# Second feed-forward net of a two-layer encoder: one more pair of blocks in seven-product form, and the down projection of eight inner blocks as seven products over both halves of the sequence

## The chip, the cores and the metric

The kernel runs on one core of one Trainium2 chip. Its time is the device time of one execution in microseconds. The core has a matrix engine (TensorE, PE in the profile), a vector engine (DVE), a scalar engine (ACT), GpSimd (POOL) and SyncE (SP), which here only issues transfers (DMAs). Each engine works through its own list of instructions in order.

## The reference

A sequence of 1024 rows of width 1024 passes through two layers and a final norm:

```
for layer in range(2):
    h = h + mixer(rms_norm(h, mix_norm[layer]))       # layer 0: gated mixing and pooling; layer 1: RWKV-7
    h = h + swiglu(rms_norm(h, ffn_norm[layer]), w_gate[layer], w_up[layer], w_down[layer])
return rms_norm(h, final_norm)

swiglu(x) = (silu(x @ w_gate) * (x @ w_up)) @ w_down      # 1024 -> 2816 -> 1024
```

The RWKV-7 mixer carries a state along the sequence, chunk by chunk; it is called the recurrence here. Everything is float32.

## The kernel before

**Tiles.** Activations lie transposed: 128 features by 512 positions is a tile, so the sequence has two halves (h = 0 and 1), the width has 8 tiles (m) and the inner width of 2816 has 22 blocks (f), or 11 pairs of blocks (i = 0 to 10). Every float32 operand is split in two parts, hi and lo, and a product of 128 x 128 by 128 x 512 is three matmuls (hi·hi, lo·hi, hi·lo): lines 441 to 443 (`mm3`) and 777 to 779 (`quarter`, four such products). A split costs one copy on ACT (`whi`, L161) and one subtraction on DVE (`wlo`, L162).

**Weights** are fetched in a fixed list (`plan`, filled by `push`, emptied by `take`), 512 KB at a time on ACT's queue, and split ahead of use. `dests` names where the split parts go; `whl` is the ordinary pair of buffers.

**Seven-product form.** Gate and up projections of most pairs are computed as a 2 x 2 block product with seven products in place of eight: the 2 x 2 is two halves of the inputs' features and two halves of the sequence (columns), and the weights' four quarters (a11 to a22) are combined on DVE (`weights` in `full_steps`: s1 to s4), as are the inputs (t1 to t4). Combining the inputs is done once for all pairs: in `combine1`, four steps, each of four loads of stored normed rows (`rl`, L2262), four subtractions (`rt`, L2267) and four splits into the tiles of `x["t1"]` to `x["t4"]`, beside the plain products of `plain_b`. A product that needs the first half alone (`first1`) is made early, beside the recurrence, and its result kept in `p1_d`.

**The second net, in order of time.** (1) The recurrence of the second half of the sequence, 1562 to 1760 us: its small matmuls wait for each other through DVE and ACT, and `drive` interleaves dense work between them: gate and up of the last of the first half's blocks, their downs, and the first products (`first1`) of four units (`AHEAD_IN`; a unit is the gate or the up of a pair). At its end the recurrence normalises (`ysb`, with a reciprocal root on POOL, `var` L446) and turns its outputs (`sm<-ident,ysb`). (2) Two more units of `first1`, the mixer's output projection, the other units. (3) `plain_b`, 1845 to 1957: gate and up of the second half for blocks 0 to 9 (pairs 0 to 4), beside `combine1`. (4) `full_steps(UNITS, ...)`, 1957 to 2124: pairs 5 to 10 in seven-product form for both halves. The hidden blocks go out to `hid1_d`. (5) `last_downs`, 2124.5 to 2317: the down projection by pairs of blocks, both halves for pairs 5 to 10, the second half alone for pairs 0 to 4 (the first half's were done beside the recurrence). Each tile of outputs is one PSUM bank, filled by 6 matmuls and added to the resident h by DVE (`residual`, L540: `h<-h,mm` for the second half, `ahi<-ahi,mm` for the first, which lies in an old tile of that name). Five PSUM banks rotate. The second half's h is brought back from `hs_d` at the stage's start (`reload`, L1960). (6) The last pair is done by `final_down` with outputs by rows, then the final norm.

A scheduler sets each engine's list of instructions at build time, so the order on DVE and SP beside PE's is fixed. All engine lists are the same as before up to a point in the recurrence of the second half at about 1690 us; everything moved lies behind that.

## Time and profile before

| | us |
|---|---|
| median of 3 runs | 2331.52 (2330.39 to 2339.88) |
| profiled execution, its own time | 2329.14 |
| its span in the profile | 2327.4 |
| PE busy | 2270.2 (98%) |
| DVE busy | 1547.3 (66%) |
| ACT busy | 957.1 (41%) |
| last stage (5), 2124.5 to 2317 | 192.5 |
| end of the last matmul stage to end of span | 10.4 |

The profile counts an engine as busy while an instruction of it runs; matmuls overlap each other, so the duration of one (389 ns in the table of lines) is longer than the distance between two starts. Idle time of PE is followed by an arrow and the engine and tile that ended it.

### The profile page before, as it was taken

How to read it: one execution, taken by the hardware profiler on the slowest of the kernel's cores; microseconds unless marked ns; L12 is line 12 of the kernel's file. 1: busy time of each engine (PE TensorE's matmuls, PEld its weight loads, DVE VectorE, ACT ScalarE, POOL GpSimd, SP SyncE). 2: the span in 40 equal slices, each digit the busy share in tenths (PEclk: the TensorE clock that was granted, in tenths of full speed). 3: DMA queues.
4: the chain of work that ended last, by engine and by line, in shares of the span. 5: the costliest groups of instructions: out<-in, count | busy, mean ns of one | idle time of the engine just before them, and what ended most of it. 6: DMA issues, size and time to landing. Idle time of an engine off the chain costs nothing.

```text
span 2327.4 us, 37995 instructions
## 1 busy us (share of the span) xinstructions
PE 2270.2 (98%) x15171; PEld 1855.4 (80%) x15171; DVE 1547.3 (66%) x2500; ACT 957.1 (41%) x1527; POOL 181.7 (8%) x207
## 2 busy tenths in 40 slices
PE   8999999999999999999998999998999999999998
PEld 6888888888888788787786788786778888888886
DVE  6435775656567976875778957775766665776565
ACT  6233444434223665533345765532333442332024
POOL 0200000000000012110110011200100000000002
PEclk9999999999999999999998999999999999999999
DMA  5114473332676466786545376775557674546342
GB/s 180 53 46 145 136 204 118 99 127 95 252 250 223 143 198 156 190 242 172 173 136 157 117 217 158 196 240 157 165 154 231 224 235 133 177 156 255 127 164 98
DMA packets 427393, 389.70 MB, mean 167 GB/s; under 512 B 99280, under 2 KB 358480, under 8 KB 424272
## 3 DMA queue, kind: packets, MB, share of 16 engines
q1 hardware_dynamic: 183120, 206.09, 27.7%
q10 hardware_dynamic: 241664, 173.30, 25.1%
q0 software_dynamic: 2432, 7.88, 1.3%
q8 instruction: 119, 1.95, 0.3%
q14 instruction: 58, 0.48, 0.1%
HBM read 281.15 MB, written 106.04 MB: 166 GB/s over the span
## 4 chain that ended last, share of the span: by engine, by line
PE 80%; DVE 11%; DMA 5%; issue 2%; ACT 1%; POOL 1%; SPq 0%; ACTq 0%; POOLq 0%; DVEq 0%
PE mm L441 14%; PE mm L442 14%; PE mm L443 14%; PE mm L777 9%; PE mm L779 9%; PE mm L778 9%; PE sm L1573 4%; DVE wlo L162 2%; DVE it L1513 1%; DVE xi L1518 1%; PE yp L1573 1%; DMA raw<-in_ffn_w_gate_dram 1%; PE mm L627 1%; PE mm L628 1%; PE mm L629 1%
## 5 line engine op out<-in xcount | busy, mean ns | idle before, releaser
L161 ACT ACTIVATE whi<-raw 128x1024 fp32r<-128x1024 f32 (+2 forms) x274 | 265.0, 975 | 401.5 <-PE mm L442 201.5
L162 DVE TENSOR_TENSOR wlo<-raw,whi 128x1024 fp32r<-128x1024 f32 (+2 forms) x274 | 307.8, 1128 | 154.3 <-ACT whi L161 119.9
L442 PE MATMUL mm<-alo,whi 128*128 128x512 f32 x864 | 341.4, 395 | 1.6 <-DVE alo L162 0.8
L441 PE MATMUL mm<-ahi,whi 128*128 128x512 f32 x832 | 331.0, 399 | 0.5 <-ACT whi L161 0.5
L443 PE MATMUL mm<-ahi,wlo 128*128 128x512 f32 x832 | 327.6, 394 | 0.5 <-DVE wlo L162 0.5
L540 DVE TENSOR_TENSOR h<-h,mm 128x512 f32<-128x512 f32 x268 | 180.2, 684 | 130.8 <-PE mm L443 127.7
L777 PE MATMUL mm<-ahi,whi 128*128 128x512 f32 x536 | 210.5, 393 | 2.3 <-DVE t L905 1.4
L778 PE MATMUL mm<-alo,whi 128*128 128x512 f32 x536 | 208.7, 389 | 0.0
L779 PE MATMUL mm<-ahi,wlo 128*128 128x512 f32 x536 | 205.3, 390 | 0.0
L442 PEld LDWEIGHTS mm<-alo,whi 128*128 128x128 f32 x864 | 162.9, 189 | 37.8 <-issue 2.6
L443 PEld LDWEIGHTS mm<-ahi,wlo 128*128 128x128 f32 x832 | 156.8, 189 | 36.0 <-issue 2.5
L441 PEld LDWEIGHTS mm<-ahi,whi 128*128 128x128 f32 x832 | 157.0, 189 | 35.5 <-issue 1.9
L441 PE MATMUL mm<-hd,dhi 128*128 128x512 f32 x368 | 144.3, 392 | 1.0 <-DVE h L540 1.0
L443 PE MATMUL mm<-hd,dlo 128*128 128x512 f32 x368 | 143.4, 390 | 0.0
L442 PE MATMUL mm<-hd,dhi 128*128 128x512 f32 x368 | 143.2, 389 | 0.0
L777 PEld LDWEIGHTS mm<-ahi,whi 128*128 128x128 f32 x536 | 100.6, 188 | 25.6 <-issue 3.2
L779 PEld LDWEIGHTS mm<-ahi,wlo 128*128 128x128 f32 x536 | 100.6, 188 | 21.1
L778 PEld LDWEIGHTS mm<-alo,whi 128*128 128x128 f32 x536 | 100.6, 188 | 21.0 <-issue 0.5
L161 ACT ACTIVATE dhi<-raw 128x1024 fp32r<-128x1024 f32 x40 | 40.6, 1053 | 170.8 <-PE mm L442 131.3
L161 ACT ACTIVATE hid<-t 128x512 fp32r<-128x512 f32 x58 | 36.5, 629 | 115.0 <-DVE t L875 113.3
L441 PEld LDWEIGHTS mm<-hd,dhi 128*128 128x128 f32 x368 | 69.1, 188 | 16.1 <-DVE h L540 1.6
L443 PEld LDWEIGHTS mm<-hd,dlo 128*128 128x128 f32 x368 | 69.1, 188 | 14.4
(446 smaller groups left out, 4706.2 us busy)
## 6 DMA issues: line engine op xcount, KB each, us to landing
raw<-in_ffn_w_down_dram ACTq DMA_DIRECT2D x76, 512.0 KB
raw<-in_ffn_w_gate_dram ACTq DMA_DIRECT2D x68, 512.0 KB
raw<-in_ffn_w_up_dram ACTq DMA_DIRECT2D x68, 512.0 KB
hid_d<-hid SPq DMA_DIRECT2D x68, 512.0 KB
hd<-hid_d SPq DMA_DIRECT2D x56, 512.0 KB
ar<-ab_d SPq DMA_DIRECT2D x16, 1024.0 KB
raw<-in_ab_w_in_dram ACTq DMA_DIRECT2D x16, 512.0 KB
raw<-in_ab_w_out_dram ACTq DMA_DIRECT2D x16, 512.0 KB
```

The source lines that it names most:

```text
L161: act.activation(hi, src, AF.Copy)
L162: (eng or dve).tensor_tensor(out=lo, in0=src, in1=hi.bitcast(F32), op=ALU.subtract)
L441: pe.matmul(o, whi, xhi, start=first, stop=False)
L442: pe.matmul(o, whi, xlo, start=False, stop=False)
L443: newest[0] = pe.matmul(o, wlo, xhi, start=False, stop=last).ins
L540: dve.tensor_tensor(out=H[h][:, m, :], in0=H[h][:, m, :], in1=o, op=ALU.add)
L627: pe.matmul(ops[j], xhi[:, k, sl], whi[:, kk], start=(k == 0), stop=False)
L628: pe.matmul(ops[j], xhi[:, k, sl], wlo[:, kk], start=False, stop=False)
L777: pe.matmul(o, wh[:, k, :], x[0][:, k, :], start=st, stop=False, skip_group_check=True)
L778: pe.matmul(o, wh[:, k, :], x[1][:, k, :], start=False, stop=False, skip_group_check=True)
L779: pe.matmul(o, wl[:, k, :], x[0][:, k, :], start=False, stop=k == 3, skip_group_check=True)
L1573: i = f(*args, **kw)
```

## The change

Pair 4 (blocks 8 and 9) joins the seven-product pairs (`LATER`), so `plain_b` covers blocks 0 to 7 only, `full_steps` takes 14 units and not 12, the first half's blocks 8 and 9 leave the dense work beside the recurrence, and two units of `first1` are made there in addition (`AHEAD_IN` 6). The down projection of the last stage is rearranged: first pair 8 (`EARLY_D`) in the old form for both halves, then blocks 0 to 7 for the second half by columns of the weights (`four_downs`: one PSUM bank takes four blocks, 12 matmuls), then blocks 8 to 15 for both halves as seven products (`eight_downs`), then pair 9 and, as before, the last pair in `final_down`. The seven-product part needs combinations of the hidden blocks 8 to 15: `keep_hidden` writes these blocks unsplit to `hf_d`, and `combine2` loads them, four at a time, into the old tiles chi and clo, subtracts and splits; `drive` interleaves it with the early downs. Hidden blocks are loaded four at a time (`load_four`).

```diff
-LATER = (5, 6, 7, 8, 9, 10)
-AHEAD_IN = 4
+LATER = (4, 5, 6, 7, 8, 9, 10)
+AHEAD_IN = 6
...
+    def keep_hidden(h, f, s, to):
+        if to is hid1_d and F4 <= f < F4 + 8:
+            sp.dma_start(hf_d[h][:, f - F4], s)
...
-        for fd in range(2 * LATER[0]):
+        for fd in range(F4):
...
     reload(hb_pool, 1, hs_d[1])
-    fgb = fin_pool.tile([P, D], F32, name="fgb")
+    x["b11"] = parts_of([low[1], low[1]], slice(0, 4))[:1] + parts_of([low[1]], slice(4, 8))
+    x["b21"] = [xd.tile([P, 4, HT], F32R, tag=t, name="d" + t) for t in ("hi", "lo")]
+    for f0, n in ((0, "b21"), (4, "b22")):
+        load_four(x[n], 1, f0)
...
+    def four_downs(f0, xs):
+        for i in range(4):
+            wh, wl = (t.rearrange("p (k c) -> p k c", k=4) for t in take(("DB", f0, i)))
+            for j in range(2):
+                js = slice(j * P, (j + 1) * P)
+                o = mmt()
+                for k in range(4):
+                    mm3(o, wh[:, k, js], wl[:, k, js], xs[0][:, k, :], xs[1][:, k, :], k == 0, k == 3)
+                residual(2 * i + j, 1, o)
+                yield 0.5
+
+    def early_downs():
+        yield from pair_downs(EARLY_D)
+        load_four(x["b11"], 0, F4)
+        yield from four_downs(0, x["b21"])
+        load_four(x["b21"], 0, F4 + 4)
+        yield from four_downs(4, x["b22"])
+        load_four(x["b22"], 1, F4 + 4)
+
+    def combine2():
+
+        def put(name, k, a, b):
+            t = nt.tile([P, HT], F32, tag="nsq", bufs=2, name="ht")
+            dve.tensor_tensor(out=t, in0=a, in1=b, op=ALU.subtract)
+            split(t, *(y[:, k, :] for y in x[name]))
+            return t
+
+        def rows_of(k):
+            ts = [c[:, 2 * (k % 2) + q, :].bitcast(F32) for c in cs for q in range(2)]
+            for t, (h, kk) in zip(ts, ((1, k), (0, k), (1, k + 4), (0, k + 4))):
+                sp.dma_start(t, hf_d[h][:, kk])
+            return ts
...
+            t1 = put("t1", k, b12, b11)
+            yield 1.0
+            t2 = put("t2", k, b22, t1)
+            yield 1.0
+            put("t4", k, b21, t2)
+            yield 1.0
+            put("t3", k, b22, b12)
+            yield 1.0
+
+    def eight_downs():
+        prev = None
+        for i in range(4):
+            a = mmt()
+            w = take(("Dn0", i))
+            quarter(a, parts_of(w, LO), x["b11"], True)
+            residual(2 * i, 0, a)
+            o = mmt()
+            quarter(o, parts_of(w, HI), x["b21"], True)
+            residual(2 * i, 0, o)
...
+    drive(early_downs(), combine2(), 2.0)
+    eight_downs()
...
+    exhaust(pair_downs(LATE_D, turn_a))
```

The line numbers of the changed program are 17 to 29 higher at the places shown below: L557 is `residual`, L1600 the recurrence's small matmuls, L2414 the subtraction of `combine2`, L2421 its loads, L1989 `reload`.

**PE, end of the second half's recurrence.** `ident,ysb` are the turns of normalised outputs, `ident,ar` those of another operand; the rows with 128x512 are dense work. Before:

```order
L1573 MATMUL yp_16532<-uv_15895,gt_15898 64x64 x16
L1573 MATMUL sm_16642<-ident_63,ar_16302 128x128 x4
L1573 MATMUL sm_16648<-ident_63,ar_16302 128x128 x4
L1573 MATMUL sm_16654<-ident_63,ysb_15856 128x128
L443 MATMUL mm_15944<-ahi_13443,wlo_15642 128x512
L441 MATMUL mm_15944<-ahi_13443,whi_15641 128x512
L442 MATMUL mm_15944<-alo_13444,whi_15641 128x512
```

The row of a dense matmul that comes last here is the third of 22 ahead of the second turn of `ysb`. In the changed program the same place reads:

```order
L1600 MATMUL yp_16400<-uv_15932,gt_15935 64x64 x16
L1600 MATMUL sm_16510<-ident_63,ar_16275 128x128 x4
L1600 MATMUL sm_16516<-ident_63,ar_16275 128x128 x4
L1600 MATMUL sm_16522<-ident_63,ysb_15896 128x128
L460 MATMUL mm_16002<-hidhi_15239,wdlo_15210 128x512
L1600 MATMUL sm_16522<-ident_63,ysb_16260 128x128
```

One dense matmul is left between the first turn and the second, and in the same way 42 of 70 are left ahead of the recurrence's last eight turns, and 24 of 48 between those and the output projection.

**DVE, start of the last stage.** Before, the additions to h follow each other, with splits of weights (`dlo`) between them:

```order
L540 TENSOR_TENSOR h_19651<-h_19651,mm_19787 128x512
L162 TENSOR_TENSOR dlo_19954<-raw_19809,dhi_19953 128x1024
L540 TENSOR_TENSOR h_19651<-h_19651,mm_19795 128x512
L540 TENSOR_TENSOR ahi_18383<-ahi_18383,mm_19823 128x512
L540 TENSOR_TENSOR ahi_18383<-ahi_18383,mm_19831 128x512
L540 TENSOR_TENSOR ahi_18383<-ahi_18383,mm_19839 128x512
```

In the changed program (ht are `combine2`'s differences, alo with ht their splits; in brackets what a row waits for):

```order
L2414 TENSOR_TENSOR ht_19758<-clo_18119,chi_18118 128x512 [waits DVE_49]
L2414 TENSOR_TENSOR ht_19796<-chi_18118 128x512 [waits DMAHW7_49,DMAHW2_49,DVE_49]
L162 TENSOR_TENSOR alo_17457<-ht_19758,ahi_17456 128x512 [waits Activation_49]
L162 TENSOR_TENSOR alo_17455<-ht_19796,ahi_17454 128x512 [waits Activation_49]
L2414 TENSOR_TENSOR ht_19814<-clo_18119,ht_19796 128x512 [waits DMAHW3_49,DVE_49]
L2414 TENSOR_TENSOR ht_19838<-clo_18119,ht_19814 128x512 [waits DMAHW1_49,DVE_49]
L162 TENSOR_TENSOR alo_17455<-ht_19814,ahi_17454 128x512 [waits Activation_49]
L162 TENSOR_TENSOR alo_17457<-ht_19838,ahi_17456 128x512 [waits Activation_49]
L2414 TENSOR_TENSOR ht_19856<-clo_18119,chi_18118 128x512 [waits DVE_49]
L162 TENSOR_TENSOR alo_17457<-ht_19856,ahi_17456 128x512 [waits Activation_49]
L557 TENSOR_TENSOR h_19578<-h_19578,mm_19686 128x512 [waits DMAHW6_49,PE_49]
L557 TENSOR_TENSOR h_19578<-h_19578,mm_19702 128x512 [waits PE_49]
```

The last but one row shown is the first addition to the second half, of the stage's ninth tile. The addition of the eighth tile stands 16 rows ahead of it, and the 15 rows between them are all `combine2`'s. From `combine2`'s first subtraction, the one at the ninth tile is 33 rows away: 12 subtractions, 12 splits, 8 additions, and a split of the stage before.

**SP, start of the last stage.** In the changed program the second half's h is brought back (`h_19578<-hs_d1_92`) behind loads of `combine2` that wait for DVE and a load of hidden blocks (alo) that waits for PE:

```order
L2421 DMA clo_18119<-hf_d0_95 128x512 [waits DMAHW3_49,DMAHW1_49,DVE_49]
L2421 DMA chi_18118<-hf_d1_96 128x512 [waits DVE_49]
L2421 DMA clo_18119<-hf_d1_96 128x512
L2421 DMA chi_18118<-hf_d0_95 128x512 [waits DMAHW4_49,DVE_49]
L2358 DMA alo_18115<-hid1_d0_89 128x4x512 [waits DMAHW5_49,PE_49]
L1989 DMA h_19578<-hs_d1_92 128x4096 [waits DMAHW6_49]
L2358 DMA dhi_19580<-hid1_d1_90 128x4x512 [waits DMAHW7_49]
L2358 DMA dlo_19581<-hid1_d1_90 128x4x512 [waits DMAHW0_49]
L2421 DMA clo_18119<-hf_d0_95 128x512 [waits DMAHW1_49,DVE_49]
```

Before, this load stood ahead of the last two stores of the stage before, in which nothing of the last stage was waited for:

```order
L790 DMA hid1_d1_90<-hid_19473 128x1024 [waits DMAHW0_49,DVE_49]
L790 DMA hid1_d1_90<-hid_19593 128x1024 [waits DMAHW3_49,DVE_49]
L1960 DMA h_19651<-hs_d1_92 128x4096 [waits DMAHW5_49,PE_49,Pool_49]
L790 DMA hid1_d0_89<-hid_19611 128x1024 [waits DMAHW6_49,DVE_49]
L790 DMA hid1_d1_90<-hid_19629 128x1024 [waits DMAHW7_49,DVE_49]
L2326 DMA hd_19667<-hid1_d0_89 128x1024 [waits DMAHW0_49]
```

The reload has moved behind the start of the last stage, and 2 MB of hidden blocks and a part of `combine2`'s loads stand behind it on the same queue.

## The prediction

> **What bounds the kernel now.** I read the page from the top: busy times, then the chain that ended last.

> ```profile
> span 2327.4 us, 37995 instructions
> PE 2270.2 (98%) x15171; PEld 1855.4 (80%) x15171; DVE 1547.3 (66%) x2500; ACT 957.1 (41%) x1527; POOL 181.7 (8%) x207
> PE 80%; DVE 11%; DMA 5%; issue 2%; ACT 1%; POOL 1%; SPq 0%; ACTq 0%; POOLq 0%; DVEq 0%
> ```

> PE bounds the whole, so a matmul less is time less wherever PE never waits. The view by stretches of time says where that is: recurrence, first products with the output projection, plain products, seven-product blocks, down projection.

> ```profile
> core 0: us, PE busy (x) PEld busy (x) DVE busy (x) ACT busy (x) POOL busy (x), PEclk, DMA share, GB/s
> 1562.00:1760.00 198.00, 187.99 (x3104) 151.88 (x3103) 123.96 (x273) 67.59 (x131) 21.77 (x10) 0.98 0.59 170
> 1760.00:1822.00 62.00, 62.00 (x278) 51.44 (x277) 29.95 (x41) 22.49 (x30) 0.00 (x0) 1.00 0.65 209
> 1845.00:1957.00 112.00, 112.00 (x495) 92.74 (x495) 63.49 (x85) 44.53 (x63) 0.00 (x0) 1.00 0.66 214
> 1957.00:2124.30 167.30, 165.00 (x723) 134.91 (x722) 124.59 (x196) 58.27 (x93) 0.00 (x0) 1.00 0.50 166
> 2124.50:2317.00 192.50, 192.50 (x881) 159.41 (x879) 120.00 (x171) 41.60 (x70) 10.80 (x12) 1.00 0.44 157
> ```

> Everywhere behind the recurrence PE is covered to the last few tenths, and DVE has 62% in the last stage. What the change can lose is therefore cover: PE can only get worse there. The price of a matmul is its distance to the next, not its duration; the timeline of PE in the last stage:

> ```profile
> 2189.79 0.39 PE L441 MATMUL mm<-hd,dhi 128*128 128x512 f32 x1
> ...
> 2192.06 0.39 PE L442 MATMUL mm<-hd,dhi 128*128 128x512 f32 x1
> ```

> Ten steps in 2.27 us: 0.227 us each, not the 0.39 of the duration column.

> **Term 1, matmuls removed.** Counted from the code: pair 4 gives up 96 matmuls beside the recurrence and 96 among the plain products, gets 48 first products and 120 in the seven-product stage: 24 fewer. Its 48 down matmuls for the first half move from beside the recurrence into the last stage, where the seven products over blocks 8 to 15 take 336 in place of 384: the last stage stays at 816, and the 48 are gone from beside the recurrence. Together 72 fewer, 72 x 0.227 = -16.3 us. (By the duration it would be -28; the bound from below is the distance, since PE runs gapless.)

> **Term 2, cover of the recurrence.** The dense work beside the last three bursts is what shrinks. Three places run short. First, the second turn of ysb: before, 22 dense matmuls bridged it.

> ```profile
> 1711.27 0.33 PE L1573 MATMUL sm<-uv,bkt 128*64 128x64 f32 x2 [0.64 <-ACT uv L1696]
> 1716.27 0.30 PE L1573 MATMUL sm<-ident,ysb 128*128 128x128 f32 x1
> 1718.08 0.69 DVE L1802 TENSOR_TENSOR ysb<-ysb,vch 128x512 f32<-128x512 f32 x1
> ```

> DVE finished the operand at 1718.77, 2.5 us after the first turn; one dense matmul and the turn cover 0.3. That is +2.2, and the wait at 1711.27 (1.0 from the start of the matmul ahead), whose cause, a split of weights ahead of uv on ACT, is gone from there in the new order, gives 1.0 back: +1.2. Second, the last eight turns. The chain behind the last state product (yp) was:

> ```profile
> 1741.81 1.15 PE L1573 MATMUL yp<-uv,gt 128*64 128x64 f32 x30
> 1742.99 0.60 ACT L1724 ACTIVATE ysb<-yp 128x512 f32<-128x512 f32 x1 [0.94 <-PE yp L1573]
> 1743.62 1.11 DVE L1777 BATCH_NORM_STATS2 st<-ysb 128x6 f32<-128x64 f32 x8 [2.66 <-ACT ysb L1724]
> 1745.85 2.90 POOL L446 TENSOR_TENSOR var<-var,small 128x16 f32<-128x16 f32 x1 [20.02 <-DVE var L1787]
> 1748.69 1.62 POOL L2224 DMA_DIRECT2D yl<-y_d  x2
> 1750.90 2.75 ACT L1794 ACTIVATE ysb<-ysb,mean,var 128x64 f32<-128x64 f32 x8
> 1754.47 0.68 DVE L1801 TENSOR_TENSOR ysb<-ysb,lnw 128x512 f32<-128x512 f32 x1
> 1755.07 0.68 DVE L540 TENSOR_TENSOR h<-h,mm 128x512 f32<-128x512 f32 x1
> 1758.89 1.03 PE L1573 MATMUL sm<-ident,ysb 128*128 128x128 f32 x8
> ```

> Through POOL's end 5.8 us (1742.96 to 1748.75), then without other work between 2.75 on ACT and four DVE steps at 0.6 (the distance of the two DVE rows): 11.1. The cover is 42 matmuls, 9.5, with 0.3 around them: +1.3. Third, the output projection: 24 matmuls (5.4 us) stand between the turns and its first product, which needs yl, and its load is issued behind POOL's reciprocal.

> ```profile
> DMA to landing us min/median/max: 8.1/9.3/10.4
> L161 ACT ACTIVATE ahi<-yl x4: 827/836/839, 1765.9 to 1770.1; 128x768 fp32r<-128x768 f32 x4
> L162 DVE TENSOR_TENSOR alo<-yl,ahi x4: 950/952/957, 1766.8 to 1771.6; 128x768 fp32r<-128x768 f32 x4
> ```

> From yp's end that is 5.8 + 0.8 + 10 to the landing and 1.8 for one copy and one subtraction, some 18.5 to 19, against 11.1 + 0.8 of turns + 5.4 = 17.3 for PE: +1.5, and I take +2.1 as four splits follow each other. With +0.3 for three thinner gaps inside the bursts (9 matmuls where 10 to 23 stood, 2.04 us of cover against waits of 1.6 to 2.1) term 2 is +4.9. Ends: +2.5 if only the last turns and the output projection count, +9 if each of the three thin gaps also waits for a DVE step and a copy that stand ahead (1.3 each).

> **Term 3, start of the last stage.** In DVE's list 33 instructions lie between combine2's first subtraction and the first addition to the second half, tile 9, 15 of them together. Tiles take PE 6 x 0.227 = 1.36 us and five banks rotate, so PE stops at the fourteenth tile's start, 13 x 1.36 = 17.7 us into the stage, until tile 9 is added. The nearest rows for combine2 are those of combine1, which does the same on other data, and for loads the reload of h:

> ```profile
> L2262 SPq DMA_DIRECT2D rl<-nb_d x4: 319/400/1488, 1846.9 to 1858.2; - x4
> 1854.35 0.69 DVE L2267 TENSOR_TENSOR rt<-rl 128x512 f32<-128x512 f32 x1 [2.45 <-DMA rl<-n_d]
> 1867.15 0.68 DVE L2267 TENSOR_TENSOR rt<-rl 128x512 f32<-128x512 f32 x1
> 1877.92 0.69 DVE L2267 TENSOR_TENSOR rt<-rl 128x512 f32<-128x512 f32 x1 [0.52 <-DMA rl<-n_d]
> 2122.02 0.32 SPq L1960 DMA_DIRECT2D h<-hs_d  x1
> 2124.50:2134.50 10.00, 10.00 (x46) 8.27 (x45) 7.20 (x11) 3.48 (x4) 0.00 (x0) 1.00 0.97 374
> ```

> combine2's loads into chi and clo can start when the seven-product stage has read these for the last time, the stage's time 0; 1 MB at 374 GB/s is 2.8, some 4 us with the issue (combine1's first rows took 7.5 from issue to use, 1846.9 to 1854.35, behind other loads: the upper end). Then 33 DVE steps at 0.6 are 19.8, at 0.69 dependent 22.8; with 0.7 for the addition and waits for ACT's copies I take 25.7. The other leg gives the same: on SP the reload stands behind a load that waits for combine2's thirteenth DVE step or so (some 12.6 us) and for tile 8 on PE (10.9), so it is issued near 13.5, where it used to be at -2.5; 1 MB of hidden blocks and its own 2 MB at 374 GB/s take 8 us and 2 to 3 of latency: 24 to 25. So PE waits 25.7 - 17.7 = +8. Ends: +4.5 (both legs 3.5 earlier, DVE at 0.6 without a wait) and +18 (combine1's pace, below). What is late next: the lo split of the four-block weights stands on DVE behind a subtraction that needs a load from behind those 4 MB, and tile 16's addition: +1. A wait of this size has a price of its own, seen after PE's 5.17 us at the recurrence's start:

> ```profile
> 1576.38 0.65 PE L1573 MATMUL sm<-XT,gt 32*32 32x32 f32 x32 [5.17 <-DMA XT<-xi_d]
> 1577.98 0.63 PE L443 MATMUL mm<-hidhi,wdlo 128*128 128x512 f32 x1
> 1578.40 0.63 PE L441 MATMUL mm<-hidhi,wdhi 128*128 128x512 f32 x1
> ...
> 1580.54 0.41 PE L443 MATMUL mm<-hidhi,wdlo 128*128 128x512 f32 x1
> 1580.79 0.40 PE L441 MATMUL mm<-hidhi,wdhi 128*128 128x512 f32 x1
> ```

> Eight matmuls went at 0.43 before the distance fell to 0.24: 8 x 0.2 = +1.6. [...] Shorter waits in the recurrence (the 1.0 at 1711.27) show no such rows here.

> **Term 4, the rest.** combine2's 16 subtractions and 16 splits, the weight combinations of pair 4 and of the down blocks (some 28 more DVE rows, 19 us) lie where DVE has 38% free and no tile waits, but for the place above: 0. The seven-product downs add to h from banks that are still accumulating, as the seven-product stage does now with 2.3 us of PE's 167 lost: for a stretch of 76 us, +0.5 (ends 0 and 2). The extra stores of unsplit blocks (4 MB, 16 issues of 0.32 on SP) lie in stages with DMA shares of 0.50 to 0.66: 0. The gain vector's later load and the tail after 2317 are unchanged in form: 0.

> **Sum.** -16.3 + 4.9 + 8 + 1 + 1.6 + 0.5 = -0.3, against the profiled execution's own 2329.1: 2328.8. The median of the runs is 2.4 above that execution, so the same sum against it is 2331.2; I say 2330. A measurement of this kernel can tell about 0.5% from no change, 11.7 us.

> **Rivals.**
> - *The cover holds* (faster). Beside combine1 PE had 112.00 of 112.00 us: the same 16 subtractions and splits cost nothing there. Against it: there no addition to h stood behind them on DVE. If DVE reached tile 9 by 18 us (33 steps in 14 us, 0.42 each, or an order in time that I misread) and only term 2 stayed near its lower end, the time is 2329.1 - 16.3 + 2.5 + 0.5 = 2316. Chance 0.20.
> - *combine2 at combine1's pace* (slower). Its steps took 12.8 and 10.8 us (starts 1854.35, 1867.15, 1877.92), its first rows 7.5 to use. Three steps stand ahead of tile 9: 7.8 + 30 = 38, PE would wait 20 and not 8: 2330 + 12 = 2342. It decides from about 37 us on. For it: the loads here share the queue with 5 MB, and two buffers (not four) hold the differences. Against it: combine1 was paced by PE's own progress, being interleaved with splits for it, and DVE had waits there that this list lacks. Chance 0.10.
> - *No change in time*, as summed: 0.70, with 2321 to 2338 as its own range (terms 2 and 3 at their near ends: -6, +8).

> **Range and chances.** Holding the near half of the faster rival and part of the slower one: 2316 to 2341. Faster by over 0.5% 0.20, within 0.70, slower 0.10.

> **What would show it.** Right, if the changed profile has 72 fewer 128x512 matmuls, PE's idle in the last stage rises from 0 to about 8 in one wait for DVE's addition to h, with matmuls at about 0.63 right behind it, and the recurrence with its turns waits some 5 more for ysb and yl. Wrong to the good side, if the first 40 us of the last stage show PE busy throughout; to the bad side, if the reload of h lands later than 30 us into that stage, or if PE also waits in the seven-product downs for splits of their weights.

## The result, and the profile after

The changed kernel took 2360.03 us (median of 4 runs, 2356.22 to 2362.84) against 2332.76 of the kernel before on the same chip (4 runs): a ratio of 1.0116, 95% interval 1.0102 to 1.013. It is 27 us slower, outside the range of 2316 to 2341. The profiled execution took 2356.22, 27.1 more than the one before.

The page first, the lines of the span and of the busy engines:

```profile
span 2354.5 us, 37850 instructions
PE 2265.1 (96%) x15099; PEld 1846.1 (78%) x15099; DVE 1554.0 (66%) x2528; ACT 972.4 (41%) x1559; POOL 180.0 (8%) x207
```

PE has 72 matmuls less, as counted, but a longer span. The view by stretches, in the stages of the prediction's table (recurrence, first products with output projection, plain products, seven-product blocks, down projection), has the same columns:

```profile
1564.00:1742.00 178.00, 164.58 (x2946) 131.54 (x2943) 110.63 (x255) 63.03 (x126) 22.17 (x10) 0.98 0.64 179
1742.00:1830.00 88.00, 86.12 (x380) 70.47 (x380) 49.02 (x68) 35.21 (x50) 1.03 (x1) 1.00 0.68 216
1830.00:1920.00 90.00, 90.00 (x399) 74.51 (x397) 55.12 (x76) 37.57 (x55) 0.00 (x0) 1.00 0.69 229
1920.00:2140.00 220.00, 199.19 (x843) 160.29 (x842) 143.54 (x227) 66.59 (x106) 0.00 (x0) 0.98 0.47 154
2140.00:2345.00 205.00, 195.53 (x881) 160.76 (x879) 127.13 (x190) 59.92 (x102) 10.77 (x12) 0.98 0.46 159
```

The fourth row is new: PE idles 20.8 us of 220 in the seven-product stage, where it had idled 2.3 of 167. The list of what PE waited for, its three largest, in us in total, times and longest:

```profile
PE mm L794 <- DVE t L932: 20.1, 11, 3.5
PE mm L458 <- DVE h L557: 12.2, 5, 9.2
PE sm L1600 <- DVE ysb L1829: 7.3, 5, 2.1
```

The second has the wait at the start of the last stage as its longest, 9.2 (the other four lie earlier); the third is the recurrence, where the kernel before has 5.8 in four waits. Both were forecast. The first was not. L932 is the addition (`now`) of a kept first product to a bank that is still accumulating; before, its rows were 1.4 us in two waits:

```profile
PE mm L777 <- DVE t L905: 1.4, 2, 1.1
```

One of the eleven waits, in the timeline of PE (start, duration, line, operands, and in brackets the idle time and what ended it):

```profile
2074.18 0.61 PE L796 MATMUL mm<-ahi,wlo 128*128 128x512 f32 x2
2076.62 0.65 PE L794 MATMUL mm<-ahi,chi 128*128 128x512 f32 x1 [1.83 <-DVE t L932]
2077.06 0.63 PE L795 MATMUL mm<-alo,chi 128*128 128x512 f32 x1
...
2080.37 0.39 PE L794 MATMUL mm<-ahi,chi 128*128 128x512 f32 x1
```

and in that of DVE:

```profile
2074.55 0.69 DVE L866 TENSOR_TENSOR s<-raw 128x512 f32<-128x512 f32 x1 [1.37 <-issue]
2075.27 0.69 DVE L868 TENSOR_TENSOR raw<-raw 128x512 f32<-128x512 f32 x1
2075.88 0.68 DVE L932 TENSOR_TENSOR t<-t,mm 128x512 f32<-128x512 f32 x1
```

A bank takes the t2, then the t3, then the t4 products of a unit (12 matmuls each), and behind each part DVE must read the bank before PE goes on in it. Here PE waits with the t4 products (`ahi,chi`) for the read behind the t3 products. Between the two PE's list has nothing but one matmul, while DVE's list has two steps of weight combination ahead of the addition, and DVE stood idle for 1.37 us ahead of the first. Six of the eleven waits are of this kind, 7.9 us in all. In the other five, 12.2 us with the three longest, PE waits with the t3 products for the read behind the t2 products. One of them, in the timeline of DVE:

```profile
2019.08 0.69 DVE L866 TENSOR_TENSOR s<-raw 128x512 f32<-128x512 f32 x1 [2.30 <-DMA raw<-in_ffn_w_gate_dram]
...
2021.61 0.68 DVE L932 TENSOR_TENSOR t<-t,mm 128x512 f32<-128x512 f32 x1
```

and in that of PE:

```profile
2022.35 0.80 PE L794 MATMUL mm<-ahi,whi 128*128 128x512 f32 x1 [3.34 <-DVE t L932]
```

The combination of the next weights (L866) stands ahead of the addition and waits for their load. So it is in four of the five; in the last, at 2122.35, DVE waits 1.87 for the load of the kept first product. The combination stood about as near before, but DVE waited less for its loads; the waits in the stage, before and changed:

```profile
DVE s L841 <- DMA raw<-in_ffn_w_gate_dram: 2.7, 4, 0.9
DVE s L866 <- DMA raw<-in_ffn_w_gate_dram: 9.3, 5, 2.5
```

Both lists are fixed when the kernel is built, and here they differ from those before. Counted in the lists, the matmuls that stand between a bank's t3 and t4 products, unit by unit of the seven-product stage:

```
before                            23 34 23 34 23 34 23 34 23 34 12 24
changed                           23 34 23  5 23  1 23  1 23  1 23  4  0 12
before + stores from t1 to t4     23 34 23  4 23  1 23  1 23  1 12 24
before + stores from h            23 34 23 34 23 34 23 34 23 34 12 24
changed, three buffers            23 34 24 24 24 24 24 24 24 24 24 24 23  0
```

and between its t2 and t3 products:

```
before                            36 16 58 16 58 16 58 16 58 16 58 12
changed                           36 16 58 31 94 59 48 62 48 62 48 35 48 24
```

So the six waits of the first kind have 0 to 5 matmuls of cover, and the five of the second kind came in spite of 48 to 94. Why the weights land late there is not separated. In three of the four places the load took 5.1 to 5.8 us from its issue (3.9 and 4.1 at two such places before). The next load of weights was issued 1.5 to 2.2 us behind it (3.6 before). In two of the three, new stores were issued within 3 us of it; in the third, ahead of the wait at 2091.72, the last new store lay 33 us back.

The third row of the first list is the kernel before with nothing but new stores; that led to the experiments. Losses by stage below are the sum over steps between matmuls above 0.3 us of what exceeds 0.227: 28.8 us in this stage (3.6 before), 12.3 in the first 110 us of the last (0 in its first 90 before).

### The profile page after: what moved, and what is told of

It is laid out like the page before. It is cut to its first block, busy times and chain, and to the rows that moved or that the text cites. A ratio compares the mean times of both kernels' runs of the same rounds, so it can differ in the third digit from the quotient of the medians.

```text
span 2354.5 us, 37850 instructions
## 1 busy us (share of the span) xinstructions
PE 2265.1 (96%) x15099; PEld 1846.1 (78%) x15099; DVE 1554.0 (66%) x2528; ACT 972.4 (41%) x1559; POOL 180.0 (8%) x207
## 5 line engine op out<-in xcount | busy, mean ns | idle before, releaser
L161 ACT ACTIVATE whi<-raw 128x1024 fp32r<-128x1024 f32 (+2 forms) x294 | 280.8, 963 | 460.5 <-PE mm L459 217.9
L162 DVE TENSOR_TENSOR wlo<-raw,whi 128x1024 fp32r<-128x1024 f32 (+2 forms) x294 | 326.3, 1115 | 152.7 <-ACT whi L161 126.1
L459 PE MATMUL mm<-alo,whi 128*128 128x512 f32 x864 | 342.6, 397 | 1.6 <-DVE alo L162 1.3
L458 PE MATMUL mm<-ahi,whi 128*128 128x512 f32 x800 | 318.4, 399 | 1.9 <-ACT ahi L161 1.4
L460 PE MATMUL mm<-ahi,wlo 128*128 128x512 f32 x800 | 314.7, 394 | 0.5 <-DVE wlo L162 0.5
L794 PE MATMUL mm<-ahi,whi 128*128 128x512 f32 x624 | 246.1, 395 | 13.6 <-DVE t L932 12.2
L795 PE MATMUL mm<-alo,whi 128*128 128x512 f32 x640 | 250.8, 392 | 0.0
L796 PE MATMUL mm<-ahi,wlo 128*128 128x512 f32 x624 | 239.4, 392 | 0.0
L557 DVE TENSOR_TENSOR h<-h,mm 128x512 f32<-128x512 f32 x228 | 153.5, 684 | 123.0 <-PE mm L460 104.6
L161 ACT ACTIVATE chi<-raw 128x512 fp32r<-128x512 f32 x64 | 39.0, 628 | 100.9 <-PE mm L795 80.5
L161 ACT ACTIVATE hid<-t 128x512 fp32r<-128x512 f32 x57 | 35.8, 628 | 88.7 <-DVE t L902 74.6
L458 PE MATMUL mm<-xhi,whi 128*128 128x512 f32 (+1 forms) x160 | 64.3, 402 | 0.0
L458 PE MATMUL mm<-hd,dhi 128*128 128x512 f32 x160 | 62.9, 393 | 1.3 <-DVE h L557 1.3
L460 PE MATMUL mm<-xhi,wlo 128*128 128x512 f32 (+1 forms) x160 | 62.7, 392 | 0.0
L460 PE MATMUL mm<-hd,dlo 128*128 128x512 f32 x160 | 62.4, 390 | 0.0
L459 PE MATMUL mm<-xlo,whi 128*128 128x512 f32 (+1 forms) x160 | 62.4, 390 | 0.0
```

Source lines behind the costliest of these rows:

```text
L161: act.activation(hi, src, AF.Copy)
L162: (eng or dve).tensor_tensor(out=lo, in0=src, in1=hi.bitcast(F32), op=ALU.subtract)
L458: pe.matmul(o, whi, xhi, start=first, stop=False)
L459: pe.matmul(o, whi, xlo, start=False, stop=False)
L460: newest[0] = pe.matmul(o, wlo, xhi, start=False, stop=last).ins
L557: dve.tensor_tensor(out=H[h][:, m, :], in0=H[h][:, m, :], in1=o, op=ALU.add)
```

## The experiments

**1. The stores alone, holding their tiles, and the same stores holding nothing.** Both are the kernel before with an added line in `save_hidden` (and the tensor `hf_d`):

```diff
+        if to is hid1_d and 10 <= f < 18:
+            sp.dma_start(hf_d[h][:, f - 10], s)                  # first kernel
+            sp.dma_start(hf_d[h][:, f - 10], H[0][:, f - 10, :])  # second kernel
```

> The kernel before, plus 16 stores of 256 KB of unsplit hidden blocks (10 to 17, both halves) from the tiles t1 to t4 in the seven-product stage; nothing else. In this build PE's list leaves 1 to 4 matmuls between the t3 products and the t4 products of the same bank in every second unit, where the kernel before has 34. Theory order (the stores hold the tiles, the list of PE is built with next to no cover for DVE's addition in between): PE waits 12 to 20 us for that addition in the stage, time 2333 + 18 = about 2350. Theory traffic (4 MB more of transfers delay the weights): also slower, 2340 to 2350, but then the next kernel too. Theory elsewhere (the loss comes from pair 4 or from what is queued on SP around it): 2333 to 2336.

> The kernel before, plus the same 16 stores at the same places, but read from the first half's resident h, which nothing overwrites in the stage: the same bytes on the same queue, no tile of t1 to t4 held. PE's list then is that of the kernel before (cover 23 and 34 in turn). Theory order: no loss, 2333 to 2337, PE's waits in the stage at 2 to 5 us. Theory traffic: as slow as the kernel with the held stores, 2340 to 2350.

The built kernels have 14 such stores, not 16: blocks 10 and 12 of the first half take another path. Twelve of the 14 held ones lie in the seven-product stage; of the changed kernel's 16 stores twelve do as well.

Measured: 2358.98 with the held stores (ratio 1.0109, 1.008 to 1.0138), 2333.51 with the free ones (0.9999, 0.9984 to 1.0015); before 2332.59. The waits for this addition in the first kernel:

```profile
PE mm L778 <- DVE t L908: 18.4, 9, 3.6
```

and in the second:

```profile
PE mm L778 <- DVE t L908: 0.8, 2, 0.5
```

Fourteen stores with no other change cost the kernel before 26 us, 28.6 of loss in the stage (3.6 before); more than the 18 that was expected. Here too most of the wait, 12.4 of 18.4, is for the read behind the t2 products. The second kernel is no full control for traffic: with nothing to wait for, the builder issued twelve of these stores one stage earlier (1870 to 1884). The next one is a better one.

**2. Three buffers, stores kept in place.** The changed kernel with

```diff
-            return fp.tile([P, HT], F32, tag=tag, bufs=2, name=tag)
+            return fp.tile([P, HT], F32, tag=tag, bufs=3 if key == "Full" else 2, name=tag)
```

> The changed kernel with three buffers in place of two for each of t1 to t4 in the seven-product stage; all stores are kept. In this build 24 matmuls stand between t3 and t4 products of a bank in every unit. Theory order: PE's loss in the stage (28.8 us of longer steps in the changed kernel, waits and slow clock together) falls to 3 to 6, the rest stays (12 at the start of the last stage), time 2360 - 23 = about 2337. Theory traffic: the stage stays at 20 or more, time 2355 to 2360.

Measured: 2329.95, ratio to before 0.9995 (0.9983 to 1.0008), 30 us below the changed kernel and 7 below what was expected. The loss in the stage is 2.1 us; the addition is gone from the list of waits. Twelve stores, 3 MB, still go out there, so their traffic alone does not make the loss. The two forecast waits remain:

```profile
PE mm L458 <- DVE h L557: 10.4, 4, 8.3
PE sm L1600 <- DVE ysb L1829: 7.2, 5, 2.1
```

**3. No combining at the start of the last stage.**

```diff
-    drive(early_downs(), combine2(), 2.0)
+    exhaust(early_downs())
```

> The changed kernel without the loads, subtractions and splits that combine the hidden blocks 8 to 15 at the start of the last stage (the seven products read the tiles as the stage before left them); all else stays. The reload of the second half's h is then issued right behind the last store of hidden blocks. Theory of the prediction (those rows on DVE and SP delay the first addition to the second half): the 9.2 us wait and the slow matmuls behind it go, -11 to -12, time about 2348; the loss in the seven-product stage stays. Rival (the wait is the reload's own, late because its memory comes free late): 5 us or more of the wait stay, 2353 or more.

Measured: 2348.27 (1.0078, 1.005 to 1.0106), 11.8 less than the changed kernel. The long wait is gone, the loss at the start of the last stage falls from 12.3 to 0 (the 2.8 us left in the second row below lie earlier in the program), that of the seven-product stage stays (30.2):

```profile
PE mm L794 <- DVE t L932: 20.3, 12, 3.3
...
PE mm L458 <- DVE h L557: 2.8, 3, 1.7
```

So `combine2`'s rows on DVE and SP made the wait; the edit takes both away, so that it does not tell them apart. The two legs of the forecast end within 0.4 us of each other in the changed kernel: the last combining row is done at 2166.47, and DVE then waits 0.36 for the reload, which SP had issued at 2154.82, 8.65 behind the last store. The reload landed at 2166.74, 11.9 behind its issue; before it took 9.7 (2122.02 to 2131.70). The 2 to 3 us of latency in the forecast's second leg are the size of what short loads took in the kernel before: two of 128 KB (`uv<-v_d`), issued at 1570.90 and 1571.39, landed 2.6 and 2.7 later. The timeline of PE in the changed kernel:

```profile
2158.02 0.39 PE L460 MATMUL mm<-alo,wlo 128*128 128x512 f32 x1
2167.58 0.80 PE L458 MATMUL mm<-alo,whi 128*128 128x512 f32 x1 [9.17 <-DVE h L557]
2168.18 0.63 PE L459 MATMUL mm<-alo,whi 128*128 128x512 f32 x1
...
2172.42 0.40 PE L460 MATMUL mm<-alo,wlo 128*128 128x512 f32 x1
```

that of DVE:

```profile
2165.78 0.69 DVE L162 TENSOR_TENSOR alo<-ht,ahi 128x512 fp32r<-128x512 f32 x1 [0.70 <-ACT ahi L161]
2166.84 3.08 DVE L557 TENSOR_TENSOR h<-h,mm 128x512 f32<-128x512 f32 x5 [0.36 <-DMA h<-hs_d]
```

and that of SP:

```profile
2146.17 0.41 SPq L814 DMA_DIRECT2D hid_d<-hid  x1
...
2154.82 0.49 SPq L1989 DMA_DIRECT2D h<-hs_d  x1
```

**4. PE in the written order.** To see whether PE's list alone decides, the changed kernel with

```diff
+    with tc.manual_schedule(engines={mybir.EngineType.PE}):
         for i, _ in enumerate(steps):
```

> The changed kernel with PE's instructions of the seven-product stage kept in the order in which they are written, which leaves 12 matmuls between the t3 and t4 products of a bank, and 36 between t2 and t3, in every unit; stores and two buffers per tile as in the changed kernel, so the tiles are held as long. Theory order (PE's list alone makes the loss): PE's waits in the stage fall from 20 to 3 to 8 us, time 2338 to 2345. Rival (the held tiles delay DVE and the loads of first products whatever PE's order is; three buffers healed that): the waits stay at 15 or more, 2353 to 2360.

Measured: 2377.98 (1.0198, 1.0183 to 1.0213). Neither theory had this. All units but the last have 12 matmuls between t3 and t4, all but the first 36 between t2 and t3, and yet PE waits 33.4 us for the same addition. One of these waits in the timeline of DVE:

```profile
1998.29 0.69 DVE L866 TENSOR_TENSOR s<-raw 128x512 f32<-128x512 f32 x1 [1.76 <-DMA raw<-in_ffn_w_gate_dram]
...
2002.62 0.68 DVE L932 TENSOR_TENSOR t<-t,mm 128x512 f32<-128x512 f32 x1
```

and of PE:

```profile
2003.45 0.77 PE L794 MATMUL mm<-ahi,whi 128*128 128x512 f32 x1 [5.41 <-DVE t L932]
```

On DVE the combination of the next weights stands ahead of the addition and waits for their load; seven steps later the addition's turn comes. All but 0.8 of the 33.4 us are waits for the read behind the t2 products; the 36 matmuls in between are 8.2 us of work and did not cover it. The distance in PE's list is one part of the matter; the other is what DVE's list has ahead. It left open whether the held tiles do harm at run time as well, and two kernels answer that for the written order: those of experiment 1, both with PE in that order. In the seven-product stage their built lists for PE, DVE and ACT are row for row the same.

> The kernel before with the 16 held stores, and PE's instructions of the seven-product stage in the order in which they are written. In that stage its lists for PE, DVE and ACT are row for row those of the next kernel; only the stores on SP, which hold t1 to t4, differ. Theory hold (at run time the held tiles make additions and loads of first products late): this kernel loses 15 us or more against the next one. Theory order (only the lists decide): both take the same time within 4 us, slow or not.

> The kernel before with the 16 stores read from the resident h of the first half (nothing held; the builder issues most of them in the stage before), and PE's instructions of the seven-product stage in the order in which they are written. Theory hold: 2333 to 2340, PE's waits in the stage under 8 us. Theory order: as slow as the kernel with held stores; 25 to 35 us of waits as in the changed kernel with the written order, 2355 to 2365.

Measured: 2364.45 held (1.0147, 1.0116 to 1.0178), 2364.35 free (1.0133, 1.0107 to 1.0158). The waits for the addition, held:

```profile
PE mm L778 <- DVE t L908: 25.8, 6, 7.4
```

and free:

```profile
PE mm L778 <- DVE t L908: 26.3, 7, 5.4
```

With the same lists, held tiles cost nothing that can be measured, and 26.3 us of waits come without any new store in the stage. That the stores cost the changed kernel its time through the lists that they made the builder write is shown on these lists; for the changed kernel's own, one reading supports it: in the stage DVE waited for a new store to land once, for 1.7 us (1963.72), and PE did not wait behind it.

**5. Less dense work beside the recurrence.** The kernel of experiment 2 with

```diff
-AHEAD_IN = 6
+AHEAD_IN = 4
```

> The kernel with three buffers, but four units of first products beside the recurrence and not six: 48 matmuls of dense work move from beside the last burst and its turns to behind it, and none is left between the last burst's steps. The number of matmuls is the same. Theory cover (dense work beside the recurrence hides its chain through DVE, ACT and POOL; each matmul taken away at the end shows as its 0.227 us of wait): 48 x 0.227 = 11 us of wait more, less 2 as the output projection's wait for yl is covered then: +7 to +11 on 2330, 2337 to 2341. Rival (the chain there is short and the dense work only postpones it): 2329 to 2333.

Measured: 2343.32 (1.0049, 1.0031 to 1.0068), 13 above the kernel of experiment 2, 2 beyond the upper end of the expectation. The waits for ysb rise from 7.2 to 15.8, the longest to 8.9, and the output projection no longer waits. The cover theory holds; the 11 us it was sized at fell short. The small steps inside the bare burst wait too, 2.7 us for one operand (Q) and 1.4 for another (gt), which was not priced.

```profile
PE sm L1600 <- DVE ysb L1829: 15.8, 6, 8.9
```

**6. A version with both mended.** Three buffers, and at the start of the last stage the reload first:

```diff
-    reload(hb_pool, 1, hs_d[1])
+    H[1] = Halves([...], 1)                 # eight tiles of one feature block
+    for j in range(8):
+        back = sp.dma_start(H[1].parts[j], hs_d[1][:, j : j + 1, :])
...
+    with tc.issue_after(back.ins):
         for f0, n in ((0, "b21"), (4, "b22")):
             load_four(x[n], 1, f0)
...
-    drive(early_downs(), combine2(), 2.0)
+    exhaust(pair_downs(EARLY_D))            # taken out of early_downs
+    drive(early_downs(), combine2(), 2.2)   # without raised priority
```

> The changed kernel with three buffers as in the run before with them, and in addition: the reload of the second half's h in eight pieces, the loads of hidden blocks for the second half issued behind it, and the combining of hidden blocks written beside the four-block downs without its raised priority. On DVE the first addition to the second half then stands ahead of most of the combining, and on SP the reload right behind the last store of hidden blocks. Theory of the prediction (place on DVE and SP makes the wait at the start of the last stage): the 8 to 9 us wait and the 2 us of slow matmuls behind it go, 2330 - 10 = 2320, if combining ends in time for the seven products. Rival (the 9 MB of loads in the first 40 us bound that start, in whatever order): PE waits as long a little later, for combined blocks or for weights, 2328 to 2332.

Measured: 2319.68 (0.9944, 0.9927 to 0.996). PE's wait at the start of the last stage is gone, and what it waits for in the whole last stage is 0.5 us of a late load and 0.2 of a turn:

```profile
PE mm L459 <- DMA dlo<-hid_d: 0.5, 1, 0.5
```

A second time, beside a control that gives the kernel before three buffers too:

> The kernel before with three buffers for each of t1 to t4 in the seven-product stage and nothing else: a control for what the third buffer is worth by itself. The kernel before loses 3.6 us to longer steps in that stage, so it can gain that at most: 2329 to 2334 if the buffer only heals what the stores did; 2325 or less would mean that part of the gain of the changed kernel with three buffers and an early reload is the buffer's own.

> The changed kernel with three buffers and the reload ahead, a second time and in more rounds, on the same chip as the control: 2319 to 2321, 0.993 to 0.996 of the kernel before, and 10 or more below the control, if the 72 matmuls are what it is faster by.

Measured: 2328.04 for the control (0.9998, 0.9988 to 1.0009), 2319.73 for the mended version (0.9966, 0.9952 to 0.998), where the kernel before took 2328.84 on this chip. The third buffer is worth nothing that can be measured by itself. The mended version beats the kernel before by 9 to 13 us of the medians, and the control by 8.3, somewhat less than the 10 expected. The 72 matmuls less the recurrence's 4.2 us (table below) would make 12.1; what takes up the rest was not traced.

## Why the prediction was wrong

By the prediction's own terms, from the two profiled executions (27.1 apart; anchors are first and last matmuls of the stages):

| term | forecast | measured |
|---|---|---|
| 1, 72 matmuls | -16.3 | -16.3 (15171 to 15099, as counted; priced at 0.227) |
| 2, recurrence, turns, output projection | +4.9 | +4.2 (1.7 to the last turn, 2.5 from there to the plain products) |
| 3, start of the last stage with the slow clock | +10.6 | +12.2 (9.3 of wait, 2.4 of slow matmuls, 0.5 else) |
| 4, the rest of the last stage | +0.5 | +0.6 |
| 4, extra stores in the seven-product stage | 0 | +26.5 (25.2 of it in steps above 0.3 us) |
| parts without a change | 0 | about 0 (+2.1, -1.0, -1.1) |

The step that failed is one sentence of term 4: the extra stores of unsplit blocks "lie in stages with DMA shares of 0.50 to 0.66: 0". It priced a store as bytes and as an issue on SP, and with three buffers these cost nothing that shows (experiment 2: 2.1 us of loss in the stage). It left out that a store reads a tile which the stage uses again two units later. The builder then wrote other lists for PE and DVE, and PE waited eleven times, 20.1 us: six times for the read behind the t3 products, with 0 to 5 matmuls of cover where most of these units had 34 (7.9 us), and five times for the read behind the t2 products, which DVE reached late as it waited for a load, of weights in four of them (12.2 us). Slow matmuls behind three of these waits added some 4.7. How much of the weights' lateness comes from the order of the lists and how much from other transfers beside them stays open. Three points make the failure plain. The sum without that row was close: with the lists healed by a third buffer the time is 2329.95, and the forecast was 2330. (The measured rows without the stores add up to +0.7, so the hit to a tenth is luck; that the sum is near nothing is not.) The wrong lists could be read before the run, as those of the two quoted places were; the prediction took the order of the seven-product stage for the old one with two units more. And the sentence on what would prove the forecast wrong named the reload and the weights of the downs, not this stage.

Point by point for the rest. The second turn of ysb waited 1.59 in one wait, a step of 2.07 (+2.2 forecast), and the wait of uv, 1.0, is gone from that place, as said; the last turns did not wait themselves, but the dense work ahead of them did, 1.5 in two places; the output projection waited 1.39 and 0.49 where +2.1 stood:

```profile
1717.46 0.95 PE L1600 MATMUL sm<-ident,ysb 128*128 128x128 f32 x7 [1.59 <-DVE ysb L1829]
...
1748.82 0.50 PE L458 MATMUL mm<-ahi,whi 128*128 128x512 f32 x1 [1.39 <-ACT ahi L161]
1749.82 0.50 PE L459 MATMUL mm<-alo,whi 128*128 128x512 f32 x1 [0.49 <-DVE alo L162]
```

The wait in the last stage came at the fourteenth tile, for the ninth tile's addition, 9.2 long (8 forecast), with eleven matmuls some 0.43 apart behind it (eight forecast). Of the rivals, the faster one (the cover holds) was wrong at both forecast places. The slower one (`combine2` at `combine1`'s pace) was wrong too: the kernel became slower, but the wait that rival spoke of was 9 and not 20. The chance of 0.10 for slower was carried by the wrong mechanism.

## What to carry to other kernels

A new reader of a buffer is a change to the schedule, whatever its bytes cost: where a builder writes the engines' lists, compare the lists of every stage in which a new instruction touches a rotating tile, before pricing it. For an engine that reads a PSUM bank between two parts of an accumulation, look at both sides: how many matmuls PE has in between, and what the reading engine's list has ahead of the read. Many matmuls in between are no cover if the reader stands behind a load (36 to 94 here). A stall of this kind may be mended by one more buffer (here 6 KB per partition and 30 us).

## What the runs showed of the hardware

Waits much shorter than the 5.17 us of the prediction's row were followed by slow matmuls in the changed kernel: nine at 0.43 behind 1.83 us (2076.62), seven each behind 3.34 and 3.50 (2022.35 and 2056.77), but none behind 2.30 (2091.72). In the seven-product stage this added some 4.7 us (23 matmuls at 0.2 more) to 20.8 of waits.

The granted clock in the traces says which waits cost it. In the kernel before it was 0.50 from 1573.75 to 1580.58, at the prediction's row, and 1.00 from there past 2300 us. In the changed kernel, between 1590 and 2300 us, it was 0.50 in four places: for 3.41 us from each of 2022.20, 2056.33 and 2076.81, and for 10.24 from 2162.15; elsewhere it was 1.00. The four starts lie 34.13, 20.48 and 85.34 us apart, 10, 6 and 25 times 3.413. The view by stretches of that length, cut at these edges (PE's busy time stands behind the length, the granted clock is the third number from the end):

```profile
2073.40:2076.81 3.41, 1.58 (x8) 1.00 (x7) 2.23 (x4) 0.63 (x1) 0.00 (x0) 1.00 0.60 174
2076.81:2080.23 3.42, 3.42 (x9) 2.67 (x9) 3.42 (x7) 1.15 (x2) 0.00 (x0) 0.50 0.00 0
2087.05:2090.47 3.42, 2.37 (x11) 1.63 (x9) 1.39 (x3) 0.07 (x1) 0.00 (x0) 1.00 0.89 247
2090.47:2093.88 3.41, 2.16 (x9) 1.80 (x10) 3.41 (x6) 1.26 (x2) 0.00 (x0) 1.00 1.05 413
2093.88:2097.29 3.41, 3.41 (x17) 2.81 (x15) 2.68 (x5) 1.23 (x2) 0.00 (x0) 1.00 0.92 316
```
